# Attention probabilities turned in 32x32 blocks on VectorE and moved by DMA, and the first half of the output weights in units of two k tiles

## The chip, the cores and the metric

The kernel runs on one core of a Trainium2 chip. The metric is the device time of one execution in microseconds (us). Before the change it is 920.57 us, the median of three runs that lie between 920.27 and 920.67.

## The reference

The program is an encoder trunk of two equal layers over 256 positions and 1024 channels, all in float32. A layer is a feed-forward part, a mixer, and a second feed-forward part, each added to the residual stream `x`. Only the mixer is touched:

```
h    = rms_norm(x)
q, k, v, u, g = split(h @ w_in)                  # 5 x 512 columns
a    = dilated_attention(rotary(q), rotary(k), v)  # 8 heads of 64
sg   = gelu(u) * (w_s @ layer_norm(gelu(g)) + b)   # 4 groups of 128 channels, chunks of 128 positions
x    = x + concat(rms_norm(a), rms_norm(sg)) @ w_out   # w_out: 1024 x 1024
```

The kernel computes the three dilated windows of the attention as one softmax over 256 keys with a bias per pair of positions (the log of how many of the windows contain the pair, or -1e30).

## The kernel before

**Weights.** All weight matrices come from memory as one stream of units. A unit is 4 tiles of 128x512, 1 MB; `weight_units` lists them in the order of use. `load_unit` (line 119) loads a unit by one DMA on SyncE's queue into one of three `raw` buffers. `split_unit` makes two parts of it: ScalarE writes the high part `whi` (line 133), VectorE the rest `wlo` (line 134), in two pieces of 128x1024 each. `run_ahead`, called by every `multiply`, issues loads five units ahead and splits two units ahead. A load waits until the split of the unit three before it has read its buffer.

**Products.** The activations are split in the same way into `xTh` and `xTl`. `multiply` (lines 165 to 167) takes one unit: for each of its 4 k tiles and each of the two halves `t` of the positions it issues three matmuls, high by high, high by low and low by high, so 24 for a unit, into two PSUM banks of 128x512. Its argument `among` puts other work in front of the k tile of a given index.

**The order of work.** The kernel is written with a planner: instructions are listed in program order, and a list scheduler puts them on the engines' queues, earlier ones first, later ones where an earlier one isn't ready by its own estimate of the times. Each engine then runs its queue strictly in order. Semaphores for all dependences are put in by the planner, those of the DMAs included: a DMA on SyncE's queue that waits for its data holds up all DMAs behind it.

**The mixer.** `mixer` runs per layer through

1. q, k and v, one w_in unit of each and then the other; `rotate` and `turn_qk` prepare the transposed q and k.
2. g: at index 2 of its first unit `attend(0)`, at index 1 of its second `attend(1)`. Each handles four heads: `scores` (line 565 on) into two PSUM banks, bias and maximum on VectorE (L571), exponential on ScalarE (L580), and the division by the sum on VectorE (L583). The probabilities lie in `pr[a]` with the query positions on the partitions.
3. u: `turn_probs(0)` at index 1 of its first unit. It turns the keys onto the partitions by 16 transposes of 128x128 on TensorE (L596) into four PSUM banks `pt`, which VectorE (L598) and ScalarE (L600) copy out in turn to `prT`. `turn_probs(1)` stands at index 0 of u's second unit, `values(0)` and `normalise` at index 1, `values(1)` at index 3.
4. `values(a)` multiplies `prT` by v (L627, `pav`), and ScalarE (L632) and VectorE (L633) make of it `aT`, high and low part, two k tiles of the attention's output; ScalarE squares it into `sq` (L635). `normalise` is the Gelu and layer norm of g, whose result is `vv`.
5. The output product. w_out has 8 k tiles, 0 to 3 of the attention and 4 to 7 of the gating branch, and two column halves `d`. Its units are (rows 0 to 3, d = 0), (rows 0 to 3, d = 1), (rows 4 to 7, d = 0), (rows 4 to 7, d = 1). The products `oa` of the first two use `aT`; among them stand `gate` (L690: `vv` by the spatial weights, then `sg`), `square_sums` (L673) and `turn_sg`, 8 transposes of 128x128 on TensorE. The products `os` of the last two use `sgT`. `add` (L705) scales each by its branch's inverse root and adds it to `x_sb`.

PSUM has two pools of four banks: `ps_acc` for accumulators, `ps_sc` for all the rest. In SBUF the pool `big` has one buffer to a tag: `h0` to `h5`, which the feed-forward parts use for their hidden activations, serve the mixer as `qk` (h0), `qkh` and later `aT` (h1), the two `pr` (h2, h3), the two `prT` (h4, h0), `qkl` (h5) and `sgT` (h2).

The feed-forward parts already turn their hidden activations without TensorE: `turn_blocks` (L276) uses VectorE's transpose of 32x32 blocks, four instructions for each quarter of the partitions, which write blocks of one partition group to another.

Of the kernel before, what the change touches and what calls it, by code (L numbers as in the profile page):

```python
# [10 lines left out]
F32 = mybir.dt.float32  # L11
# [37 lines left out]
def weight_units():  # L49
# [3 lines left out]
    for l in range(DEPTH):  # L53
        for f in ("ffn1", "mix", "ffn2"):
            if f == "mix":
# [4 lines left out]
                for rows in (range(4), range(4, 8)):  # L60
                    for d in (0, 1):
                        units.append((l, "w_out", rows, d))
# [25 lines left out]
def trunk_kernel(ctx: ExitStack, tc: tile.TileContext, ws, x, cxt, rows, sgw, ident, bias, rot, out):  # L88
# [80 lines left out]
    def multiply_first(accs, lhs):  # L169

        for i in range(len(accs)):
# [3 lines left out]
            for j, k in enumerate(UNITS[i][2]):  # L175
                xh, xl = lhs(k)
                wh, wl = hi[:, j * W:(j + 1) * W], lo[:, j * W:(j + 1) * W]
                for t in range(NT):
# [3 lines left out]
                    nc.tensor.matmul(accs[j][t], xl[:, s], wh, start=False, stop=False)  # L182

# [327 lines left out]
    def mixer(l, st, nxt):  # L511
# [31 lines left out]
        prT = [big.tile([P, 4, 2, S], F32, tag="h4", name="prT")]  # L543
# [47 lines left out]
        def turn_probs(a):  # L591
            for h in range(4):
                pt = ps_sc.tile([P, 2, S], F32, tag="sc", name="pt")
                for kt in range(2):
                    for t in range(NT):
                        nc.tensor.transpose(pt[:, kt, t * P:(t + 1) * P], pr[a][:, t, h, kt * P:(kt + 1) * P], id_sb)  # L596
                if h % 2:
                    nc.vector.tensor_copy(prT[a][:, h], pt)  # L598
                else:
                    nc.scalar.activation(prT[a][:, h], pt, AF.Copy)  # L600
# [13 lines left out]
        multiply(acc_g, st.lhs, True, False, {2: lambda: attend(0)})  # L614
        multiply(acc_g, st.lhs, False, True, {1: lambda: attend(1)})

# [4 lines left out]
        def values(a):  # L621
            bank = ps_sc.tile([P, 2, S], F32, tag="sc", name="pav")
            for p in range(2):
                for kt in range(2):
                    for j in range(2):
                        h = 2 * p + j
                        nc.tensor.matmul(bank[j * DH:(j + 1) * DH, p], vs[:, kt, (4 * a + h) * DH:(4 * a + h + 1) * DH],  # L627
                                         prT[a][:, h, kt], start=kt == 0, stop=kt == 1)
# [10 lines left out]
        prT.append(big.tile([P, 4, 2, S], F32, tag="h0", name="prT"))  # L639
        multiply(acc, st.lhs, True, False, {1: lambda: turn_probs(0)})  # L640
# [20 lines left out]
        def values_and_gate():  # L661
            values(0)
            normalise()

        multiply(acc, st.lhs, False, True, {0: lambda: turn_probs(1), 1: values_and_gate, 3: lambda: values(1)})
        nc.vector.tensor_tensor(sq[:, :2], sq[:, :2], sq[:, 2:], op=ALU.add)
        nc.vector.tensor_tensor(sq[:, 0], sq[:, 0], sq[:, 1], op=ALU.add)
# [151 lines left out]
```

## Time and profile before

| what | value |
|---|---|
| median of three runs | 920.57 us |
| the profiled execution | 922.07 us, its span 920.3 us |
| TensorE's granted clock, mean | 0.999 |
| TensorE busy | 912.4 us (99%) |
| VectorE busy | 751.1 us (82%) |
| ScalarE busy | 466.3 us (51%) |
| moved by DMA | 174.14 MB, 189 GB/s |
| mixer of the first layer, from its first u matmul to its first oa matmul | 236.23 to 254.84 us |

The span goes from the first to the last instruction. TensorE's matmuls are pipelined: a duration in the profile holds the way through the array too, and the next one starts before it ends, so the distance between starts is what a matmul costs. Times in a timeline count from the span's start. The second layer's mixer looks like the first's, 453 us later.

### The profile page before, as it was taken

The page shows a single profiled execution, that of the slowest core. Times are in us where ns is not written, and L with a number is a line of the kernel's source. Part 1 is how long each engine was busy: PE and PEld are TensorE (multiplying, and loading weights), DVE is VectorE, ACT ScalarE, POOL GpSimd, SP SyncE. Part 2 cuts the span into 40 slices and gives each one's busy share as a digit, 9 for nine tenths or more (in the row PEclk, how much of TensorE's full clock was granted, in tenths as well). Part 3 has the DMA queues.
Part 4 walks back from the last instruction along what each step waited for, and adds up shares of the span by engine and source line. Part 5 has one row for each costly group of instructions (what it writes and reads, how often), then busy time and mean ns, then how long its engine had stood idle before and what let it go on. Part 6 is the DMA issues. An engine that isn't in the chain of part 4 may idle for free.

```text
span 920.3 us, 11062 instructions
## 1 busy us (share of the span) xinstructions
PE 912.4 (99%) x4178; PEld 750.2 (82%) x4178; DVE 751.1 (82%) x1203; ACT 466.3 (51%) x654; POOL 21.5 (2%) x48
## 2 busy tenths in 40 slices
PE   9999999999999999999999999999999999999997
PEld 6888888888778888888888888888887888888886
DVE  6698996796789699896687998966887887998854
ACT  6544544356756544434445544445467545444440
POOL 0000000000010000000000000000000100000000
PEclk9999999999999999999999999999999999999999
DMA  8765555565334645646555555455543455565351
GB/s 330 297 259 183 187 201 205 187 217 192 138 113 175 215 141 206 219 147 237 192 197 177 192 213 191 152 209 208 201 140 135 164 202 183 183 210 200 126 195 47
DMA packets 26982, 174.14 MB, mean 189 GB/s; under 512 B 3120, under 2 KB 4272, under 8 KB 6960
## 3 DMA queue, kind: packets, MB, share of 16 engines
q1 hardware_dynamic: 26496, 172.86, 52.6%
q8 instruction: 33, 0.54, 0.2%
q10 hardware_dynamic: 432, 0.56, 0.2%
q14 instruction: 21, 0.17, 0.1%
HBM read 172.36 MB, written 1.05 MB: 188 GB/s over the span
## 4 chain that ended last, share of the span: by engine, by line
PE 97%; DVE 1%; issue 1%; ACT 0%; DMA 0%; POOL 0%; POOLq 0%; DVEq 0%
PE down L165 8%; PE down L166 8%; PE down L167 8%; PE gate L166 7%; PE up L166 7%; PE up L167 7%; PE gate L167 7%; PE up L165 7%; PE gate L165 7%; PE both L166 2%; PE both L165 2%; PE both L167 2%; PE g L165 1%; PE q L167 1%; PE g L166 1%; PE os L165 1%
## 5 line engine op out<-in xcount | busy, mean ns | idle before, releaser
L134 DVE TENSOR_TENSOR wlo<-raw,whi 128x1024 fp32r<-128x1024 f32 (+2 forms) x325 | 378.4, 1201 | 105.1 <-ACT whi L133 102.8
L133 ACT ACTIVATE whi<-raw 128x1024 fp32r<-128x1024 f32 (+2 forms) x325 | 322.4, 1039 | 246.9 <-issue 100.1
L276 DVE STREAM_TRANSPOSE turned<-h 32x256 f32<-32x256 f32 (+1 forms) x384 | 158.9, 414 | 6.3
L167 PE MATMUL down<-whi,hT 128*128 128x512 f32 x340 | 132.3, 389 | 0.0
L165 PE MATMUL down<-whi,hT 128*128 128x512 f32 x340 | 132.3, 389 | 0.0
L166 PE MATMUL down<-wlo,hT 128*128 128x512 f32 x340 | 132.3, 389 | 0.0
L167 PE MATMUL gate<-whi,xTl 128*128 128x512 f32 x304 | 118.3, 389 | 0.0
L167 PE MATMUL up<-whi,xTl 128*128 128x512 f32 x304 | 118.3, 389 | 0.0
L166 PE MATMUL gate<-wlo,xTh 128*128 128x512 f32 x304 | 118.3, 389 | 0.0
L165 PE MATMUL up<-whi,xTh 128*128 128x512 f32 x304 | 118.3, 389 | 0.0
L166 PE MATMUL up<-wlo,xTh 128*128 128x512 f32 x304 | 118.3, 389 | 0.0
L165 PE MATMUL gate<-whi,xTh 128*128 128x512 f32 x304 | 118.1, 389 | 0.0
L167 PEld LDWEIGHTS down<-whi,hT 128*128 128x128 f32 x340 | 63.8, 188 | 13.3
L165 PEld LDWEIGHTS down<-whi,hT 128*128 128x128 f32 x340 | 63.8, 188 | 13.3
L166 PEld LDWEIGHTS down<-wlo,hT 128*128 128x128 f32 x340 | 63.8, 188 | 13.2
L279 ACT ACTIVATE hT<-turned 128x512 fp32r<-128x512 f32 x44 | 26.8, 626 | 80.2 <-DVE turned L276 80.2
L165 PEld LDWEIGHTS gate<-whi,xTh 128*128 128x128 f32 x304 | 57.1, 188 | 11.9
L165 PEld LDWEIGHTS up<-whi,xTh 128*128 128x128 f32 x304 | 57.1, 188 | 11.9
L166 PEld LDWEIGHTS up<-wlo,xTh 128*128 128x128 f32 x304 | 57.1, 188 | 11.9
L166 PEld LDWEIGHTS gate<-wlo,xTh 128*128 128x128 f32 x304 | 57.1, 188 | 11.9
L167 PEld LDWEIGHTS up<-whi,xTl 128*128 128x128 f32 x304 | 57.1, 188 | 11.8
L167 PEld LDWEIGHTS gate<-whi,xTl 128*128 128x128 f32 x304 | 57.0, 188 | 11.8
(172 smaller groups left out, 1064.7 us busy)
## 6 DMA issues: line engine op xcount, KB each, us to landing
raw<-in_ws SPq DMA_DIRECT2D x154, 1024.0 KB, 4.8
raw<-in_ws SPq DMA_DIRECT2D x8, 512.0 KB, 3.2
raw<-in_ws SPq DMA_DIRECT2D x7, 256.0 KB, 5.5
x_sb<-in_x SPq DMA_DIRECT2D x1, 1024.0 KB, 10.8
ln_sb<-in_rows SPq DMA_DIRECT2D x1, 1024.0 KB, 7.4
out<-y SPq DMA_DIRECT2D x2, 320.0 KB, 2.5
xt_sb<-in_cxt SPq DMA_DIRECT2D x1, 512.0 KB, 7.9
sgw_sb<-in_sgw SPq DMA_DIRECT2D x1, 512.0 KB, 6.5
```

The source lines that it names most:

```text
L133: nc.scalar.activation(hi[:, s], raw[:, s], AF.Copy)
L134: nc.vector.tensor_tensor(lo[:, s], raw[:, s], f32(hi[:, s]), op=ALU.subtract)
L165: nc.tensor.matmul(acc[t], xh[:, s], wh, start=start and j == 0, stop=False)
L166: nc.tensor.matmul(acc[t], xh[:, s], wl, start=False, stop=False)
L167: nc.tensor.matmul(acc[t], xl[:, s], wh, start=False, stop=stop and j == len(ks) - 1)
L276: nc.vector.transpose(to[32 * c:32 * c + 32, :, :, b, :], frm[32 * b:32 * b + 32, :, :, c, :])
L279: nc.scalar.activation(dst_hi, src, AF.Copy)
```

## The change

The probabilities leave TensorE. `turn_probs(a)` is now two VectorE instructions, one for each half of the query positions, that transpose all 32x32 blocks of a 128x1024 tile in place of their partition group (`prB`), and 16 DMAs on SyncE's queue from SBUF to SBUF that carry blocks to the partition group where they belong: one DMA for each pair of source group `b` and target group `c`, 32 partitions of 2 KB. All of a half's DMAs need both VectorE instructions, and a product of `values` needs all 16. `turn_probs(0)` now stands in program order behind g's first unit, `turn_probs(1)` behind its second. `values` reads the probabilities as its moving operand in runs of 32 elements. The buffers change: `prB` in h4 and h0, `prT` in h2 and h3 (where `pr` was), `sgT` in h5.

The first half of w_out comes in two units of two k tiles by both column halves. `multiply_pairs` runs through such a unit: k and k + 1 for d = 0, then for d = 1. So both halves' accumulators are open together (all four banks of `ps_acc`), and k tiles 2 and 3, which depend on `values(1)`, are first used in the second of the two units.

The order among the products changes with it: `normalise` stands ahead of u's second unit, `values(0)` at index 3 of it, `gate` at index 2 of the first pair unit, `values(1)` at index 0 of the second, `turn_sg` at its index 1, `square_sums` with the attention's inverse root at its index 3. All four `add`s of `oa` come behind it, and the first `os` accumulators take banks of `ps_sc`.

```diff
@@ weight_units
-                for rows in (range(4), range(4, 8)):
-                    for d in (0, 1):
-                        units.append((l, "w_out", rows, d))
+                for k in (0, 2):
+                    units.append((l, "w_out_pair", ((k, 0), (k + 1, 0), (k, 1), (k + 1, 1)), 0))
+                for d in (0, 1):
+                    units.append((l, "w_out", range(4, 8), d))
@@ trunk_kernel
+    def multiply_pairs(accs, lhs, start, stop, among):
+        i = done["used"]
+        done["used"] += 1
+        run_ahead(i + 1)
+        hi, lo = splits.pop(i)
+        for j, (k, d) in enumerate(UNITS[i][2]):
+            if j in among:
+                among[j]()
+            xh, xl = lhs(k)
+            wh, wl = hi[:, j * W:(j + 1) * W], lo[:, j * W:(j + 1) * W]
+            for t in range(NT):
+                s = slice(t * P, (t + 1) * P)
+                nc.tensor.matmul(accs[d][t], xh[:, s], wh, start=start and j % 2 == 0, stop=False)
+                nc.tensor.matmul(accs[d][t], xh[:, s], wl, start=False, stop=False)
+                nc.tensor.matmul(accs[d][t], xl[:, s], wh, start=False, stop=stop and j % 2 == 1)
@@ mixer
         def turn_probs(a):
-            for h in range(4):
-                pt = ps_sc.tile([P, 2, S], F32, tag="sc", name="pt")
-                for kt in range(2):
-                    for t in range(NT):
-                        nc.tensor.transpose(pt[:, kt, t * P:(t + 1) * P], pr[a][:, t, h, kt * P:(kt + 1) * P], id_sb)
-                if h % 2:
-                    nc.vector.tensor_copy(prT[a][:, h], pt)
-                else:
-                    nc.scalar.activation(prT[a][:, h], pt, AF.Copy)
+            tmp = big.tile([P, 4, 16, 32], F32, tag=("h4", "h0")[a], name="prB")
+            for t in range(NT):
+                nc.vector.transpose(tmp[:, :, 8 * t:8 * t + 8].rearrange("p c q j -> p q c j"),
+                                    pr[a][:, t].rearrange("p h (k c i) -> p (h k) c i", c=4, i=32))
+            dst = big.tile([P, 4, 16, 32], F32, tag=("h2", "h3")[a], name="prT")
+            for b in range(4):
+                for c in range(4):
+                    nc.sync.dma_start(dst[32 * c:32 * c + 32, b], tmp[32 * b:32 * b + 32, c])
+            prT.append(dst)
...
         multiply(acc_g, st.lhs, True, False, {2: lambda: attend(0)})
+        turn_probs(0)
         multiply(acc_g, st.lhs, False, True, {1: lambda: attend(1)})
+        turn_probs(1)
...
-                        nc.tensor.matmul(bank[j * DH:(j + 1) * DH, p], vs[:, kt, (4 * a + h) * DH:(4 * a + h + 1) * DH],
-                                         prT[a][:, h, kt], start=kt == 0, stop=kt == 1)
+                        probs = prT[a].rearrange("p b (t q) j -> p q t b j", t=NT)[:, 2 * h + kt]
+                        nc.tensor.matmul(bank[j * DH:(j + 1) * DH, p].rearrange("p (t b j) -> p t b j", t=NT, b=4),
+                                         vs[:, kt, (4 * a + h) * DH:(4 * a + h + 1) * DH], probs,
+                                         start=kt == 0, stop=kt == 1)
...
-        multiply(acc, st.lhs, True, False, {1: lambda: turn_probs(0)})
+        multiply(acc, st.lhs, True, False)
...
-        multiply(acc, st.lhs, False, True, {0: lambda: turn_probs(1), 1: values_and_gate, 3: lambda: values(1)})
+        normalise()
+        multiply(acc, st.lhs, False, True, {3: lambda: values(0)})
...
-        for d in (0, 1):
-            acc = accumulators("oa")
-            multiply(acc, a_lhs, True, True, {1: gate, 3: square_sums} if d == 0 else {0: turn_sg})
-            if d == 0:
-                r_a = inverse_root(ssq_a, DA)
-            add(acc, d, r_a)
+        accs = [accumulators("oa") for _ in range(2)]
+        multiply_pairs(accs, a_lhs, True, False, {2: gate})
+        r_a = []
+        def root_first():
+            square_sums()
+            r_a.append(inverse_root(ssq_a, DA))
+        multiply_pairs(accs, a_lhs, False, True, {0: lambda: values(1), 1: turn_sg, 3: root_first})
+        for d in (0, 1):
+            add(accs[d], d, r_a[0])
         r_s = inverse_root(ssq_s, DG)
         new = nxt()
         for d in (0, 1):
-            acc = accumulators("os")
+            acc = accumulators("os", ps_sc, "sc") if d == 0 else accumulators("os")
             multiply(acc, s_lhs, True, True)
```

The sums of `sq` move into `square_sums`, and the host's stream of weights gets the tiles of the pair units in their new order.

More of the change, by code (lines that the diff above doesn't have):

```diff
@@ L542, in mixer @@
         pr = [big.tile([P, NT, 4, S], F32, tag=f"h{2 + a}", name="pr") for a in range(2)]
-        prT = [big.tile([P, 4, 2, S], F32, tag="h4", name="prT")]
+        prT = []
         mx = small.tile([P, NT, 2, H], F32, tag="mx", name="mx")
@@ L638, in mixer @@
         acc = accumulators("u")
-        prT.append(big.tile([P, 4, 2, S], F32, tag="h0", name="prT"))
-        multiply(acc, st.lhs, True, False, {1: lambda: turn_probs(0)})
+        multiply(acc, st.lhs, True, False)
         vv = big.tile([P, NT, W], F32, tag="vv", name="vv")
@@ L659, in normalise @@
                                                op0=ALU.mult, op1=ALU.add)
-        def values_and_gate():
-            values(0)
-            normalise()
-        multiply(acc, st.lhs, False, True, {0: lambda: turn_probs(1), 1: values_and_gate, 3: lambda: values(1)})
-        nc.vector.tensor_tensor(sq[:, :2], sq[:, :2], sq[:, 2:], op=ALU.add)
-        nc.vector.tensor_tensor(sq[:, 0], sq[:, 0], sq[:, 1], op=ALU.add)
+        normalise()
+        multiply(acc, st.lhs, False, True, {3: lambda: values(0)})
         ssq_a = small.tile([P, NT, 1], F32, tag="ssq_a", name="ssq_a")
         def square_sums():
+            nc.vector.tensor_tensor(sq[:, :2], sq[:, :2], sq[:, 2:], op=ALU.add)
+            nc.vector.tensor_tensor(sq[:, 0], sq[:, 0], sq[:, 1], op=ALU.add)
             bank = ps_sc.tile([P, NT, 1], F32, tag="sc", name="ss")
@@ L681, in mixer @@
         sg = big.tile([P, NT, W], F32, tag="sg", name="sg")
-        sgT = big.tile([P, 2, 4, S], F32R, tag="h2", name="sgT")
+        sgT = big.tile([P, 2, 4, S], F32R, tag="h5", name="sgT")
         ssq_s = small.tile([P, NT, 1], F32, tag="ssq_s", name="ssq_s")
@@ L754, in _stream @@
                      for cc in range(2) for m in ("_w_gate", "_w_up")]
+            parts.append(np.concatenate(tiles, axis=1).reshape(-1))
+            continue
+        if name.endswith("_pair"):
+            tiles = [inputs[name[:-5]][l][k * P:(k + 1) * P, d * W:(d + 1) * W] for k, d in ks]
             parts.append(np.concatenate(tiles, axis=1).reshape(-1))
```

## The prediction

> **What bounds the kernel now.** I read the profile's page first, then the chain of waits in order of time through the first layer's mixer, then the timelines of TensorE, VectorE, ScalarE and SyncE there. Page:
>
> ```profile
> span 920.3 us, 11062 instructions
> ...
> PE 912.4 (99%) x4178; PEld 750.2 (82%) x4178; DVE 751.1 (82%) x1203; ACT 466.3 (51%) x654; POOL 21.5 (2%) x48
> ...
> PE 97%; DVE 1%; issue 1%; ACT 0%; DMA 0%; POOL 0%; POOLq 0%; DVEq 0%
> ```
>
> TensorE is busy 99% of the span and 97% of the chain that ends last is its own work. So an instruction taken off TensorE is worth its share of the stream, and any new wait in front of TensorE costs its full length. In the mixer the chain goes through the lines of the change (start, length, what):
>
> ```profile
> 237.76 1.75 PE pt L596 x16
> ...
> 243.60 1.75 PE pt L596 x16
> ...
> 246.72 1.88 PE pav L627 x16
> 248.60 0.43 PE u L165
> ...
> 258.54 1.96 PE mixed L690 x8
> ```
>
> Two blocks of 16 probability transposes (L596) stand on the chain in this layer, 1.75 us each; the product with the values (L627) takes 1.88, and the matmul behind it 0.43 instead of 0.23, so 2.08 in all.
>
> **What is removed.** The timeline of TensorE (start, duration, which overlaps the next one's):
>
> ```profile
> 236.23 0.39 PE L165 MATMUL u<-whi,xTh 128*128 128x512 f32 x1
> ...
> 237.36 0.39 PE L167 MATMUL u<-whi,xTl 128*128 128x512 f32 x1
> 237.60 1.91 PE L596 MATMUL pt<-id_sb,pr 128*128 128x128 f32 x16
> 239.26 0.48 PE L165 MATMUL u<-whi,xTh 128*128 128x512 f32 x1
> 239.57 0.40 PE L166 MATMUL u<-wlo,xTh 128*128 128x512 f32 x1
> ...
> 243.21 0.39 PE L167 MATMUL u<-whi,xTl 128*128 128x512 f32 x1
> ...
> 258.02 0.39 PE L167 MATMUL oa<-whi,aT 128*128 128x512 f32 x1
> ```
>
> and of the tile pt (duration min/median/max, first and last start):
>
> ```profile
> L596 PE MATMUL pt<-id_sb,pr x64: 270/272/273, 237.6 to 698.1; 128*128 128x128 f32 x64
> ```
>
> From 239.57 to 243.21 there are 16 steps of projection matmuls, 0.2275 each. From 237.36 to 239.57 are 2.21 us, of which two steps (0.455) would be there without the block: a block costs 1.755. The 64 transposes are four such blocks over two layers: **7.0 us off TensorE**. The duration of one, 272 ns, isn't its price; they overlap. The Trainium skill ("TensorE: Matmul & The Clock Gate", Part 4) gives about 275 ns for a transpose in a kernel's context; the trace has that duration, but a start every 0.104 us. Priced by that figure the gain would be 64 x 0.275 = 17.6 us, by the trace 7.0.
>
> Second, between 258.02 and 258.54 the gate's product (L690) starts 0.29 later than a step, because vv is late; in layer 2:
>
> ```profile
> 711.65 1.96 PE L690 MATMUL mixed<-vv,sgw_sb 128*128 128x256 f32 x8 [0.18 <-DVE vv L658]
> ```
>
> normalise now stands ahead of values(0) instead of behind it, so ScalarE gets to the Gelu of g sooner. I take these 0.47 us as gained too (bounds 0 and 0.47): **7.5 us** before new waits, 3.75 a layer.
>
> **What is added on VectorE.** Groups by line and shape (busy, mean ns):
>
> ```profile
> L276 DVE STREAM_TRANSPOSE turned<-h 32x256 f32<-32x256 f32 x320 | 139.6, 436 | 5.2
> ...
> L276 DVE STREAM_TRANSPOSE turned<-h 32x128 f32<-32x128 f32 x64 | 19.4, 303 | 1.1
> ...
> L598 DVE COPY prT<-pt 128x512 f32<-128x512 f32 x8 | 5.3, 681 | 0.0
> ```
>
> 128 more elements a partition cost 133 ns, so the new 128x1024 transpose takes an estimated 303 + 7 x 133 = 1.23 us; a layer has four (4.9 us) in place of four copies (2.6). TensorE doesn't feel this work itself, but it delays the probabilities:
>
> ```profile
> 232.51 1.22 DVE L583 TENSOR_TENSOR pr<-pr,sm 128x1024 f32<-128x1024 f32 x1
> 233.64 2.35 DVE L134 TENSOR_TENSOR wlo<-raw,whi 128x1024 fp32r<-128x1024 f32 x2
> ...
> 241.51 1.22 DVE L583 TENSOR_TENSOR pr<-pr,sm 128x1024 f32<-128x1024 f32 x1
> 242.66 2.35 DVE L134 TENSOR_TENSOR wlo<-raw,whi 128x1024 fp32r<-128x1024 f32 x2
> ```
>
> The first half's probabilities are normalised at 233.64. With one transpose behind them they are turned at 234.9, with both in the way at 236.1; I take 235.6, since VectorE has little idle time here. The second half's, at 242.66 now, get four transposes more ahead of them and two copies (1.28) fewer: 242.66 + 4.9 - 1.3 = 246.3; with a weight split of 2.35 slipped in, 248.6. I take 247.0.
>
> **What is added on SyncE's queue.** 16 DMAs of 64 KB for each half, and each reads both transposes, so all wait for the second. The issues of SyncE at the start, where they go back to back, and two of the mixer's:
>
> ```profile
> 0.72 1.81 SPq L119 DMA_DIRECT2D raw<-in_ws  x4
> 2.57 0.43 SPq L223 DMA_DIRECT2D xt_sb<-in_cxt  x1
> ```
>
> ```profile
> 236.02 0.33 SPq L119 DMA_DIRECT2D raw<-in_ws  x1
> 245.04 3.20 SPq L119 DMA_DIRECT2D raw<-in_ws  x2
> ```
>
> Four issues in 1.85 us are 0.46 each: the sixteenth starts 6.9 us after the first. Time from issue to landing, by kind:
>
> ```profile
> raw<-in_ws SPq DMA_DIRECT2D x154, 1024.0 KB, 4.8
> ...
> out<-y SPq DMA_DIRECT2D x2, 320.0 KB, 2.5
> ...
> raw<-in_ws SPq DMA_DIRECT2D x2, 128.0 KB, 3.3
> ...
> id_sb<-in_ident SPq DMA_DIRECT2D x1, 64.0 KB, 10.1
> ```
>
> No row moves SBUF to SBUF. The bounds are 2.5 (the stores at the end, nothing behind them) and 10.1 (64 KB as here, but issued into the crowd of the start). DMA share (last but one column) where they will run:
>
> ```profile
> 230.00:235.00 5.00, 5.00 (x40) 4.02 (x39) 4.80 (x11) 3.61 (x10) 0.00 (x0) 1.00 0.02 7
> 240.00:245.00 5.00, 5.00 (x31) 4.32 (x30) 4.97 (x8) 4.86 (x10) 0.00 (x0) 1.00 0.05 15
> ```
>
> The engines are nearly idle, so I take 2.9, between the store and the 128 KB load. The Trainium skill ("DMA: Bandwidth & Descriptors", Rules for kernel authors) speaks against transfers this small: under 64 KB one pays mostly overhead. Its fit for GpSimd's path, 2.0 us and bytes over 436e3, would make 2.15 us of one; with that the forecast below would be 914.3.
>
> **What waits behind it.** On SyncE the weight load of 236.02 now stands behind the first 16 (to about 242.9), that of 245.04 perhaps behind the second 16 (254.7). Landing in 4.8 they are there by 247.7 and 259.5. They are the second pair of w_out units, first used when the oa products end (about 265, below, and a unit later), and their split takes 2.35: both have over 2 us in hand, so I price them at nothing. If that cover were gone, each would cost its lateness one for one.
>
> **The path to the end of a layer's mixer.** Without the blocks TensorE reaches values(0), now at index 3 of u's second unit, after 42 steps: 236.23 + 42 x 0.2275 = 245.8. The last DMA starts at 235.6 + 6.9 = 242.5 and lands at 245.4 (bounds 245.0 and 252.6): just in time. Then 2.08 and 6 steps (249.2), a pair unit of 24 steps with the gate's 1.96 (256.7), and values(1), now first in the second pair unit. Its last DMA starts at 247.0 + 6.9, plus 0.4 for a weight load between, 254.3, and lands at 257.2: **0.5 us of wait** (0.1 at 2.5, 2.4 at 4.8). A wait at values(0) moves the need of values(1) too, so the two don't add.
>
> Behind values(1) stands its own consumer. Now:
>
> ```profile
> 248.65 0.47 ACT L632 ACTIVATE aT<-pav,cols_sb 128x256 fp32r<-128x256 f32 x1 [1.98 <-PE pav L627]
> ...
> 249.68 0.47 ACT L632 ACTIVATE aT<-pav,cols_sb 128x256 fp32r<-128x256 f32 x1 [0.55 <-DVE aT L633]
> ```
>
> ```profile
> 249.16 0.48 DVE L633 SCALAR_TENSOR_TENSOR aT<-pav,cols_sb,aT 128x256 fp32r<-128x256 f32 x1 [0.68 <-ACT aT L632]
> ```
>
> pav ends at 248.60; aT's high part is there at 249.12, its low part at 249.64, 1.0 later. Now six matmuls of u stand between; in the new order the next matmul uses k = 2 at once. turn_sg's 8 transposes (8 x 0.11 = 0.9) can fill it if the planner puts them there: 0.2 of wait filled, 1.0 not, I take **0.6**.
>
> The unit order of w_out, the adds of sq put later, sgT in h5 and os in the other PSUM pool add no instruction to TensorE; VectorE's four adds of oa come together at its end (4 x 0.7), under os' 24 steps (5.5). The values' moving operand is read in runs of 32 elements: at nothing, at worst twice its 1.88.
>
> Sum: 7.5 - 2 x (0.5 + 0.6) = 5.3 us. The span is 920.3 of a profiled execution of 922.07; the median of the runs is 920.57, near the span, and I take the 5.3 off the median: **915.3**.
>
> **Rivals.** *All hidden* (0.22): landing within 2.4, and the sg transposes fill the gap: 7.5 - 2 x 0.2 = 7.1, 913.5. For it: DMA shares of 0.02 and 0.05; against it: no row under 2.5.
> *VectorE is late* (0.14): the split goes ahead of the turn; 248.6 + 6.9 + 0.4 + 2.9 = 258.8, a wait of 2.1 and 1.0 for aT: 7.5 - 6.2, 919.3. For it: VectorE's 4.80 and 4.97 of 5 us.
> *The DMAs land late: slower* (0.15): values(1) waits for the sixteenth DMA. With 0.6 for aT the gain is gone when landing takes 2.4 + 3.15 = 5.5 us; midway between that and the 10.1 of the 64 KB row, at 7.8, the wait is 5.4, and 7.5 - 2 x 6.0 makes 925.1. For it: that row; against it: the idle engines.
> *The strided probabilities read slowly* (0.07): twice 1.88 in four products eats 7.5: 922.8. No row has runs of 32 on TensorE.
>
> **Numbers.** The forecast has 0.42 (its own range 914 to 917). The range goes from under the all-hidden case to past the slow reads, 912.5 to 923.0, and leaves out most of the late DMAs. Faster by over 0.2% (1.8 us, about what a measurement of this kernel tells from nothing): 0.42 and 0.22 and a third of VectorE late, 0.68; slower 0.19, same 0.13.
>
> **What would show it.** Right: L596 gone from TensorE and 4 x 1.75 from its stream; VectorE transposes of 128x1024 near 1.23 us; 16 issues some 7 us long on SyncE; TensorE idle before pav for about half a microsecond with DMA prT as releaser, and before oa for aT. Wrong: an idle of over 3 us before pav (late DMAs or VectorE: the time of the last transpose tells which), pav blocks longer than 1.88, or a wait for whi or wlo that points to starved weight loads.

## The result, and the profile after

The changed kernel takes 928.05 us (median of four executions, 927.62 to 929.3) beside 920.53 of the kernel before on the same chip: a ratio of 1.0084, 95% interval 1.0067 to 1.0102. The change makes it slower by 7.5 us, where 5.3 us faster was forecast. All times below are medians of undisturbed executions: of the ten of no_wait_for_move two, of 1009 and 2904 us, are left out. The profiled execution took 928.06. That of before had lost 1.8 us already in its first 10 us, so its span of 920.3 is too long for a comparison by spans (926.3 after); stages are compared instead. From the first matmul of u to the first of the feed-forward part behind it, the first layer's mixer takes 44.91 us before and 48.74 after, the second layer's 44.93 and 48.88. That stretch holds the whole loss.

The page of the changed kernel:

```profile
span 926.3 us, 10996 instructions
...
PE 908.0 (98%) x4114; PEld 744.6 (80%) x4114; DVE 755.4 (82%) x1203; ACT 462.5 (50%) x646; POOL 21.4 (2%) x48
```

The 64 transposes are gone (4178 matmuls before, 4114 now), yet the span grew. What TensorE waits for (in all, times, longest; the first six of the list, both layers; the third is of the start and stands in the list of before too):

```profile
PE oa L200 <- DVE aT L657: 5.3, 2, 2.7
PE oa L198 <- ACT aT L656: 2.6, 4, 0.8
PE sink L364 <- DVE warm L361: 1.2, 1, 1.2
PE pt L307 <- DVE x_sb L725: 1.0, 2, 0.5
PE pav L650 <- DVE st L673: 0.8, 1, 0.8
PE pav L650 <- DMA prT<-prB: 0.8, 1, 0.8
```

Without the line of the start these are 10.5 us, all of it new. The longest, 2.7 us a layer, is for the low part of aT, the step behind the first values. The timelines of TensorE and of VectorE there (start, duration, in brackets the idle time before it and its releaser):

```profile
246.22 1.95 PE L650 MATMUL pav<-prT,v 128*64 128x256 f32 x16 [0.76 <-DMA prT<-prB]
248.73 0.50 PE L198 MATMUL oa<-whi,aT 128*128 128x512 f32 x1 [0.56 <-ACT aT L656]
...
252.63 0.73 PE L200 MATMUL oa<-whi,aT 128*128 128x512 f32 x2 [2.71 <-DVE aT L657]
```

```profile
246.92 1.19 DVE L135 TENSOR_TENSOR wlo<-raw,whi 128x1024 fp32r<-128x1024 f32 x1
248.97 0.75 DVE L681 SCALAR_TENSOR_TENSOR vv<-vn,rs,ln_sb 128x512 f32<-128x512 f32 x1 [0.86 <-POOL rs L677]
249.64 0.75 DVE L679 SCALAR_TENSOR_TENSOR vn<-vn,mv,ln_sb 128x512 f32<-128x512 f32 x1
250.31 1.22 DVE L135 TENSOR_TENSOR wlo<-raw,whi 128x1024 fp32r<-128x1024 f32 x1
251.44 0.74 DVE L681 SCALAR_TENSOR_TENSOR vv<-vn,rs,ln_sb 128x512 f32<-128x512 f32 x1
252.10 0.48 DVE L657 SCALAR_TENSOR_TENSOR aT<-pav,cols_sb,aT 128x256 fp32r<-128x256 f32 x1
```

No matmul of u stands between the values and their consumer. The planner put u's last k tile ahead of the values. It probably took the moved probabilities to come later, by its own estimate: in three kernels below whose moves start earlier (four_moves_gate_later, no_transposes, all_relieved) that k tile stands behind the values again, in a fourth (no_division) it doesn't. No run tests this order alone. aT's high part is there at 248.67; the low part waits in VectorE's queue behind the layer norm's end, a wait for GpSimd inside it, and a weight split. VectorE has no slack to be on time. Windows of 4 us (busy time of PE, PEld, DVE, ACT, POOL, with the number of instructions; then granted clock, DMA share and GB/s), after and then before, and VectorE's first instruction of before in its last window. By the first matmul of u (234.42 after, 236.23 before), the same stage comes 1.8 us later in before:

```profile
238.00:242.00 4.00, 4.00 (x19) 3.30 (x19) 4.00 (x8) 3.78 (x14) 1.11 (x1) 1.00 0.44 100
242.00:246.00 4.00, 3.46 (x16) 2.53 (x14) 4.00 (x6) 3.99 (x6) 0.00 (x0) 1.00 0.48 107
250.00:254.00 4.00, 1.37 (x5) 0.94 (x6) 3.06 (x5) 1.39 (x3) 0.00 (x0) 0.95 0.46 114
```

```profile
238.00:242.00 4.00, 4.00 (x26) 3.56 (x25) 3.17 (x6) 4.00 (x14) 0.00 (x0) 1.00 0.53 225
250.00:254.00 4.00, 4.00 (x26) 2.56 (x25) 1.16 (x3) 3.43 (x6) 0.00 (x0) 1.00 0.47 199
```

```profile
253.32 1.28 DVE L650 BATCH_NORM_STATS2 st<-vn 128x6 f32<-128x512 f32 x2 [2.65 <-ACT vn L649]
```

Before, VectorE had caught up: it stood idle for 2.65 us up to 253.32, waiting for ScalarE, while TensorE went on without a gap (26 matmuls in the window). Now TensorE idles and waits for VectorE.

The wait also costs clock. Windows of 2 us of the changed kernel (granted clock third from the end):

```profile
252.00:254.00 2.00, 1.37 (x5) 0.94 (x6) 1.06 (x3) 1.39 (x3) 0.00 (x0) 0.91 0.45 107
254.00:256.00 2.00, 2.00 (x6) 1.52 (x6) 1.73 (x2) 1.47 (x3) 0.00 (x0) 0.50 0.44 99
256.00:258.00 2.00, 2.00 (x9) 1.70 (x7) 1.38 (x3) 0.00 (x0) 0.00 (x0) 0.74 0.43 98
```

Behind the idle 2.7 us the granted clock falls to 0.50, and a matmul starts every 0.425 us instead of 0.2275. From 253.20 to 258.24 stand seven matmuls and the gate's product, 5.04 us. At full clock they would be 7 x 0.2275 and 1.6 (its price before, without its wait for vv), 3.2 to 3.4 us: some 1.7 us are lost a layer. The windows give the same, 2 x (0.09 + 0.50 + 0.26).

SyncE's queue (start, time from first to last issue, count) and, on ScalarE, what comes of it:

```profile
234.57 10.09 SPq L619 DMA_DIRECT2D prT<-prB  x16
244.77 0.53 SPq L120 DMA_DIRECT2D raw<-in_ws  x1
245.77 11.06 SPq L619 DMA_DIRECT2D prT<-prB  x16
256.87 9.00 SPq L120 DMA_DIRECT2D raw<-in_ws  x4
```

```profile
262.06 2.01 ACT L134 ACTIVATE whi<-raw 128x1024 fp32r<-128x1024 f32 x2 [1.61 <-DMA raw<-in_ws]
263.97 0.46 ACT L656 ACTIVATE aT<-pav,cols_sb 128x256 fp32r<-128x256 f32 x1
```

The 16 issues take 10.1 and 11.1 us, and the next weight load goes out at 256.87. ScalarE waits for those weights at 262.06, and the high part of the second half's aT stands behind that split in ScalarE's queue: 0.65 us more of wait at 264.49.

By layer: 44.91 less the two blocks (3.51) and the late vv (0.29) would be 41.1, and it is 48.74. Of the 7.6 the waits of the first layer make 5.2 (0.76, 0.56, 2.71, 0.65, 0.52), the clock 1.7. Most of the remaining 0.7 went into the starts of the gating branch's transposes, now one block: they take 1.75 by the starts, 0.65 of it the wait, against 0.54 before.

### The profile page after: what moved, and what is told of

The parts are those of the page before. It is cut to its first block, busy times and chain, and to the rows that moved or that the text cites. A ratio compares the mean times of both kernels' runs of the same rounds, so it can differ in the third digit from the quotient of the medians.

```text
span 926.3 us, 10996 instructions
## 1 busy us (share of the span) xinstructions
PE 908.0 (98%) x4114; PEld 744.6 (80%) x4114; DVE 755.4 (82%) x1203; ACT 462.5 (50%) x646; POOL 21.4 (2%) x48
```

## The experiments

Four causes offer themselves: SyncE's issues and what stands behind them (A in the first texts), VectorE's queue (B), the new order in itself, and the late use of vv. The stretch given is that of the first layer, from u to the feed-forward part (before 44.91, after 48.74). In four kernels the second layer's differs by more than 1 us: turn_only 51.55, no_division 47.95, after_lo_on_pool 54.19, four_moves_gate_later 45.63.

| kernel | us | ratio to before, 95% | stretch |
|---|---|---|---|
| order_only | 923.56 | 1.0035 (1.0021 to 1.0050) | 46.59 |
| turn_only | 930.72 | 1.0109 (1.0094 to 1.0124) | 48.76 |
| no_wait_for_move | 922.63 | 1.0021 (1.0011 to 1.0031) | 45.79 |
| aT_first | 931.28 | 1.0114 (1.0095 to 1.0133) | 50.06 |
| two_queues | 934.86 | 1.0159 (1.0144 to 1.0174) | 52.12 |
| four_moves | 923.90 | 1.0032 (1.0022 to 1.0042) | 46.51 |
| four_moves_gate_later | 924.22 | 1.0046 (1.0030 to 1.0063) | 46.97 |
| before_and_transposes | 923.20 | 1.0028 (1.0018 to 1.0038) | 46.37 |
| before_and_moves | 920.51 | 1.0001 (0.9992 to 1.0010) | 44.90 |
| no_transposes | 920.87 | 1.0008 (0.9998 to 1.0017) | 45.15 |
| no_division | 923.92 | 1.0031 (1.0019 to 1.0043) | 46.14 |
| all_relieved | 917.83 | 0.9974 (0.9964 to 0.9984) | 43.62 |
| after_lo_on_pool | 938.18 | 1.0192 (1.0177 to 1.0207) | 51.82 |
| before_lo_on_pool | 929.92 | 1.0100 (1.0085 to 1.0115) | 49.09 |
| first_by_dma | 920.38 | 1.0000 (0.9990 to 1.0010) | 44.87 |
| second_by_dma | 920.80 | 1.0004 (0.9994 to 1.0013) | 45.09 |
| old_first_by_dma | 921.05 | 1.0007 (0.9997 to 1.0016) | 45.20 |
| mixed_tuned | 917.77 | 0.9972 (0.9962 to 0.9983) | 43.53 |

### The two parts of the change, each alone

`order_only`: the new order and the pair units, with the probabilities turned by TensorE.

```diff
         def turn_probs(a):
-            tmp = big.tile([P, 4, 16, 32], F32, tag=("h4", "h0")[a], name="prB")
...
+            for h in range(4):
+                pt = ps_sc.tile([P, 2, S], F32, tag="sc", name="pt")
...
-        multiply(acc, st.lhs, True, False)
+        multiply(acc, st.lhs, True, False, {1: lambda: turn_probs(0)})
-        multiply(acc, st.lhs, False, True, {3: lambda: values(0)})
+        multiply(acc, st.lhs, False, True, {0: lambda: turn_probs(1), 3: lambda: values(0)})
```

> The probabilities are turned on TensorE as before the change and copied out by VectorE and ScalarE; the pair units and the whole new order behind them (normalise, values, gate, turn_sg, adds) are kept. Theory A (the time goes to the arrival of prT: 16 issues on one queue take 10 to 11 us a half): no wait for prT is left, so only the new order's small waits in the second pair unit remain: 920.5 + 2 x 0.9 = 922. Theory B (the time goes to VectorE's queue, where the end of normalise and a weight split stand ahead of the low part of aT): that order stays, but six matmuls of u now stand between pav and oa: about 1.3 us a layer of wait and no drop of the clock, 924 to 925. Theory C (the new order costs the time by itself, whoever turns the probabilities): the change's cost of some 15 us without its gain of 7, 935.

It costs 3.0 us. Its waits:

```profile
PE oa L200 <- DVE aT L653: 1.8, 2, 0.9
...
PE pt L307 <- DVE x_sb L721: 1.1, 2, 0.5
```

Nothing but what VectorE makes is late, and with no added load on VectorE: the order alone uses up the slack that its queue had.

`turn_only`: the DMA turning, with the old units and the old places of values, gate and square sums.

```diff
+                for rows in (range(4), range(4, 8)):
+                    for d in (0, 1):
+                        units.append((l, "w_out", rows, d))
...
-        multiply(acc, st.lhs, False, True, {3: lambda: values(0)})
+        multiply(acc, st.lhs, False, True, {1: values_and_gate, 3: lambda: values(1)})
```

> The turning by VectorE and DMA alone: the output weights keep their old units and the values, the gate and the square sums their old places. The new order alone cost 3.0 us (923.6 against 920.5). If the two parts add up, this kernel takes 928.0 - 3.0 = 925.0. If the turning is a gain that only the new order spoils (the forecast's own sum less what the order was to hide), it takes 914 to 918. If the new order was what hid part of the moves, as the forecast had it, it takes more than 928, up to 932: the values are due earlier and TensorE waits for the moved copy, 2 us or more a half.

It is slower than the whole change: TensorE waits for the moves of the second half, 2.5 us in the first layer and 3.5 in the second. So the new order does hide most of the moves, as the forecast had it (0.8 us of wait is left in the changed kernel, which is 2.7 us faster than this one), and the parts don't add: +3.0 and +10.2 alone, +7.5 together.

### SyncE's queue

`no_wait_for_move`: the values read `prB`; the moves run, and nothing waits for them.

```diff
-            prT.append(dst)
+            prT.append(tmp)
```

> The changed kernel, with all its transposes and moves, but the products read the tile that VectorE's transposes wrote (blocks not moved to their partitions), so they wait for no move; what it leaves out is that the moved copy is used. Bound on what the arrival of prT costs in all. Theory A: every wait up to the first oa goes, 7 us of transposes gained and some 1 us a layer lost behind values(1): 915 to 917. Theory B: TensorE reaches aT sooner, but VectorE's queue still holds its low part: 920 or more.

`two_queues`: every second move is issued by ScalarE.

```diff
-                    nc.sync.dma_start(dst[32 * c:32 * c + 32, b], tmp[32 * b:32 * b + 32, c])
+                    (nc.sync, nc.scalar)[c % 2].dma_start(dst[32 * c:32 * c + 32, b], tmp[32 * b:32 * b + 32, c])
```

> The changed kernel, but every second of the 16 moves of a half is issued by ScalarE instead of SyncE; the computation is complete. Theory A: a half's issues take about 5 us instead of 10 to 11, prT lands some 5 us sooner, the planner finds it ready within u, and the waits of the first half (0.9 for prT, 0.6 and 2.7 for aT, 1.8 of half clock a layer) go: 928 - 2 x 5.7 = 916.7. If the issue time belongs to something the two queues share, nothing changes: 928. Theory B: only the part of the wait that u's last matmuls cover goes, 920 to 922.

`four_moves`: one DMA of 128 partitions in place of four.

```diff
-                for c in range(4):
-                    nc.sync.dma_start(dst[32 * c:32 * c + 32, b], tmp[32 * b:32 * b + 32, c])
+                nc.sync.dma_start(dst[:, b], tmp[:, b])
```

> Each half is moved by 4 DMAs of 128 partitions in place of 16 of 32; the bytes are the same, but no block changes its partitions, so the values are multiplied by a wrongly turned copy and the numbers that come out are not the reference's; the amount of work is the same. If SyncE's 32 issues a layer are the root (10.1 and 11.1 us in which the weight loads stand behind them), they take 4 x 0.59 = 2.4 us a half now, the moved copy comes 7 us sooner, the next weight loads too, and the time is 914 to 918. If VectorE's queue is the root (the copy without any wait for the move took 922.8), the time is 921 to 925, with 2 to 3 us a layer in which TensorE waits for a tile of VectorE. If it is the bytes and not the count that makes an issue long, an issue takes 2 us or more and the time stays at 927 to 929.

`four_moves_gate_later`: besides, `gate` stands behind the whole first pair unit.

```diff
-        multiply_pairs(accs, a_lhs, True, False, {2: gate})
+        multiply_pairs(accs, a_lhs, True, False, {})
+        pair_end = last[0]
...
+                    with tc.issue_after(pair_end):
+                        nc.tensor.matmul(bank[:, g], sgw_sb[:, l, g0 + g, :], vv[:, :, s], start=True, stop=True)
```

> The kernel with 4 moves a half (923.9; the moved blocks stay on their partitions, so the values are multiplied by a wrongly turned copy, with the same amount of work), and the gate's product put behind all 24 products of the first pair of output weights. There TensorE waited 2.9 us a layer for vv, its only long wait. If SyncE's issues and the place of the gate are together the whole loss, the 5.7 us go and the time is 916 to 919. If VectorE is late with whatever comes next, TensorE waits for the low parts of aT or for the turned gate instead, and the time is 921 to 925.

In the order no_wait_for_move, two_queues, four_moves and four_moves_gate_later, the first line of each list of waits, and between them ScalarE's queue in two_queues and SyncE's in four_moves:

```profile
PE mixed L710 <- DVE vv L681: 5.7, 2, 2.9
```

```profile
PE mixed L710 <- DVE vv L681: 13.5, 2, 6.8
```

```profile
234.92 5.38 ACTq L619 DMA_DIRECT2D prT<-prB  x8
240.35 0.51 ACT L598 ACTIVATE pr<-pr,mx 128x256 f32<-128x256 f32 x1 [8.20 <-DMA prT<-prB]
```

```profile
PE mixed L709 <- DVE vv L680: 5.7, 2, 2.9
```

```profile
235.38 2.47 SPq L618 DMA_DIRECT2D prT<-prB  x4
```

```profile
PE oa L202 <- DVE aT L658: 6.5, 2, 3.2
```

An issue costs 0.6 us by the count, not by the bytes (4 of 256 KB in 2.47). With the issues gone or the moves free the loss shrinks to 2 to 4 us and doesn't vanish: TensorE then waits 2.9 us a layer for vv, and with the gate out of the way 3.2 us for the low part of aT. These are two instructions of the same stretch of VectorE's queue. In two_queues TensorE no longer waits for the moves, which go out in 5.4 us instead of 10.1. But ScalarE's eight issues stand ahead of the exponentials of the second half, which start 3.1 us later than in the changed kernel, counted from u's first matmul (5.59 against 2.52), and the next eight take 5.0 us of its queue once more. In the end vv is 6.8 us late, and the kernel is slower than either account had allowed. On this the Trainium skill ("DMA: Bandwidth & Descriptors", Issuing engines are not separate DMA queues) says that issuing from several engines saves only the sequencer's time, usually small beside the transfer. For one move that is so here, 0.6 us against 2.0 from issue to landing; it is the 16 in a row, 10.1 us, that count, and on ScalarE they delay its compute.

`before_and_moves`: the kernel before with 32 unused moves a layer at the same places.

```diff
+            src = pr[a].rearrange("p t h s -> p (t h s)").rearrange("p (c q j) -> p c q j", c=4, j=32)
+            for b in range(4):
+                for c in range(4):
+                    nc.sync.dma_start(scr[b // 2][32 * c:32 * c + 32, b % 2], src[32 * b:32 * b + 32, c])
```

> The kernel before, with the 32 moves of 64 KB of each layer added on SyncE's queue, at the places where the changed kernel has them; they copy blocks of the probabilities to places that nothing reads. TensorE's work and VectorE's are as before, so only SyncE's queue and the transfers show: some 20 us of issues a layer ahead of the weight loads. If the weight loads behind them are in time all the same (priced at nothing in the prediction), 920.3 to 921. If these loads are what comes late, 922 to 927, with waits of ScalarE's split for its weights and of TensorE behind it.

In the old order SyncE's 21 us a layer cost nothing measurable, and no product of the mixer waits for weights.

### VectorE's queue

`aT_first`: in the changed kernel the end of the layer norm is issued behind the first half's low parts.

```diff
+                with tc.issue_after(low[1]):
+                    nc.vector.scalar_tensor_tensor(vn[t], vn[t], mv[:, t, 0:1], ln_sb[:, l, 0],
+                                                   op0=ALU.subtract, op1=ALU.mult)
```

> The changed kernel, with one thing moved: on VectorE's queue the end of normalise (the four instructions that make vv) stands behind the low part of the first half's aT instead of ahead of it. Turning, moves, units and TensorE's list up to the first oa are the same. Theory B: the wait of 2.7 us a layer ahead of the first high-by-low matmul of oa falls to about 0.4, and with it the time at half clock (about 1.8 us a layer): 928 - 2 x 4.1 = 920. Theory A: prT comes as late as before, and the wait only turns up elsewhere (vv and the gate are later): 926 to 928.

The wait of 2.7 is gone, and the time is worse, outside every outcome that was named. Its waits, and ScalarE in the second half:

```profile
PE oa L198 <- ACT aT L658: 7.4, 4, 3.3
PE pav L652 <- DMA prT<-prB: 4.1, 3, 1.8
```

```profile
261.91 2.00 ACT L134 ACTIVATE whi<-raw 128x1024 fp32r<-128x1024 f32 x2 [3.71 <-DMA raw<-in_ws]
```

TensorE gets to the second values earlier and meets SyncE's lateness there: the moves, and the weight split in front of aT. One queue put right exposes the other.

`before_and_transposes`: the kernel before with the eight block transposes a layer, unused.

```diff
+            for t in range(NT):
+                nc.vector.transpose(scr[t].rearrange("p c (g q) j -> p q (c g) j", g=2),
+                                    pr[a][:, t].rearrange("p h (k c i) -> p (h k) c i", c=4, i=32))
```

> The kernel before, with the eight block transposes of VectorE of each layer added at the places where the changed kernel has them; what they write is not used. TensorE's work and SyncE's are as before, so only VectorE's added load shows: 4 x 1.24 = 5.0 us a layer, half of it ahead of the end of g. If TensorE doesn't feel VectorE's queue (as the prediction had it), 920.3 to 921. If VectorE's queue is the root of the loss, 923 to 927, with new waits for tiles of VectorE behind u (the transposed probabilities, vv, aT).

2.6 us, but not in the way expected: in the mixer TensorE waits 0.2 us at most. By the starts on TensorE, u takes 0.53 us more in the first layer, the transposes 0.46, os 0.53. The planner cut TensorE's turns into more pieces (12, 4, 3, 9 and 4 instead of 16 and 16), presumably since it saw the probabilities later. So VectorE's 5 us a layer cost 1.3 us a layer even here, by the order and not by a wait.

`no_transposes`: the changed kernel without VectorE's transposes; the moves read `pr`. `no_division`: the division by the sums is left out instead, as much of VectorE. In both `gate` stands behind the first pair unit.

```diff
-            for t in range(NT):
-                nc.vector.transpose(tmp[:, :, 8 * t:8 * t + 8].rearrange("p c q j -> p q c j"),
-                                    pr[a][:, t].rearrange("p h (k c i) -> p (h k) c i", c=4, i=32))
+            tmp = pr[a].rearrange("p t h s -> p (t h s)").rearrange("p (c q j) -> p c q j", c=4, j=32)
```

> The changed kernel without VectorE's block transposes: the 16 moves a half copy the probabilities as they lie, so the values are multiplied by a copy that is turned only by blocks; the rest of the work is the same, and the gate's product stands behind the first pair of output weights. VectorE has 4 x 1.24 = 5.0 us a layer less, SyncE's 32 issues and the transfers stay. If VectorE's queue is the root, TensorE's waits for the low parts of aT go (2.7 us a layer) and with them the lowered clock (1.8 us a layer): 914 to 919. If SyncE's issues or the latency of the moves are the root, TensorE still waits for them: 923 to 928.

```diff
-            nc.vector.tensor_tensor(pr[a][:, t], pr[a][:, t], sm[:, t, 1, s][:, :, None].to_broadcast([P, 4, S]),
-                                    op=ALU.mult)
```

> The changed kernel without the division of the probabilities by their sums (4 x 1.22 = 4.9 us of VectorE a layer), all else the same, the gate's product behind the first pair of output weights. VectorE's relief lies at another place than in the kernel without the transposes, and the moves start earlier by one division. If it is VectorE's load that counts and not what VectorE does, 914 to 919 again. If it is the transposes themselves or the moves behind them, 923 to 928.

Waits of the first and of the second, and ScalarE in no_transposes:

```profile
PE oa L200 <- ACT aT L655: 3.4, 2, 1.7
PE oa L202 <- DVE aT L656: 2.5, 2, 1.2
```

```profile
PE oa L200 <- ACT aT L656: 6.0, 4, 2.5
PE oa L202 <- DVE aT L657: 2.0, 2, 1.0
```

```profile
256.91 0.63 ACT L277 ACTIVATE junk<-sg 128x512 f32<-128x512 f32 x1 [4.72 <-DVE sg L713]
...
258.16 1.99 ACT L134 ACTIVATE whi<-raw 128x1024 fp32r<-128x1024 f32 x2
```

Taking 5 us a layer off VectorE gives back 7.2 or 4.1 us, not the 9 to 14 expected. Of the waits that remain, half in the first kernel and two thirds in the second are for the high part of aT, which ScalarE makes behind a weight split. In no_transposes that split, at 258.16, waits for no weights: in ScalarE's queue it stands behind the squares of the gating branch, for which ScalarE idles 4.72 us. In no_division it waits 0.47 us for weights, too. So this is mostly the order of ScalarE's queue, as the planner set it, and only a little of it SyncE's lateness.

`all_relieved`: no transposes, and four moves a half, so both queues are relieved and the order is left. (Here the planner also puts the split ahead of those squares, and the wait for the high part is 0.2 us.)

> The changed kernel without VectorE's transposes and with 4 moves a half, which copy the probabilities as they lie (the values are multiplied by an unturned copy; the products, their sizes and their order stay), the gate's product behind the first pair of output weights. VectorE's 5 us a layer and most of SyncE's issues are gone together; only the new order is left. If these three are the whole loss, the time is 920.5 - 7.0 + 3.0 = 916.5, within 1.0: the 7.0 of the transposes left out and the 3.0 that the order alone cost. Of the waits of the kernel without transposes, the 1.7 us a layer for the high parts of aT behind a late weight split are gone. If something else is lost, 919 or more.

917.83: 1.3 above the sum, just outside what was given. The first halves' low part is still 1.2 us late a layer, and x_sb 0.5. From the changed kernel there are two ways to this one. By VectorE first, the 10.2 us split into 7.2 and 3.0 for SyncE; by SyncE first (924.2), into 3.8 and 6.4 for VectorE. These shares aren't pure. Leaving the transposes out also lets the moves start 5 us earlier; both routes move the gate behind the pair unit on their first step, which between four_moves and four_moves_gate_later changed nothing clear. The step of 6.4 is the cleanest, since TensorE waits for moves on neither side of it, and the low part's wait falls from 3.2 to 1.2 us. As much work taken off elsewhere in VectorE's queue (no_division) gave only 4.1. So VectorE's transposes are the larger share, 6.4 to 7.2 us, but where in its queue the work stands matters as much as how much it is.

### VectorE's work on GpSimd

`after_lo_on_pool` and `before_lo_on_pool`: the low parts of u's weights are made by GpSimd (the first with `gate` behind the first pair unit too).

```diff
-            nc.vector.tensor_tensor(lo[:, s], raw[:, s], f32(hi[:, s]), op=ALU.subtract)
+            eng = nc.gpsimd if UNITS[i][1] == "w_in" and UNITS[i][3] == 3 else nc.vector
+            eng.tensor_tensor(lo[:, s], raw[:, s], f32(hi[:, s]), op=ALU.subtract)
```

> The changed kernel with the low parts of the weights of u (4 of 128x1024 a layer, 4 x 1.22 = 4.9 us of VectorE) made by GpSimd, the gate's product behind the first pair of output weights; nothing is left out. No row shows what one of these takes on GpSimd. If VectorE is the root and GpSimd takes under 3 us for one, 914 to 920. If GpSimd takes over 4 us for one, the exponentials of the second half, whose negated maxima stand behind two of them, come late, and the time is over 928. If VectorE is not the root, 925 to 929.

> The kernel before with the same low parts of the weights of u made by GpSimd. If TensorE is what bounds the kernel before, as the prediction had it (waits of VectorE under 0.5 us a layer), the time stays at 920 to 921. If GpSimd is slow enough to hold up the exponentials, it is over 922. Below 919 VectorE was felt before too.

GpSimd's groups and ScalarE's timeline in the first:

```profile
L136 POOL TENSOR_TENSOR wlo<-raw,whi 128x1024 fp32r<-128x1024 f32 x8 | 21.0, 2653 | 71.5 <-ACT whi L134 71.5
```

```profile
238.56 0.51 ACT L601 ACTIVATE pr<-pr,mx 128x256 f32<-128x256 f32 x1 [5.10 <-POOL mx L598]
```

2.65 us for one, under the 3 that was to be enough, but two of them stand ahead of the negated maxima, and ScalarE idles 5.1 us ahead of the exponentials (0.27 in the changed kernel). Counted from u's first matmul they start 0.9 us later than there; in the other kernel 2.5 later than before. One division on VectorE beside GpSimd's work also took 3.44 us instead of 1.22. The kernels are 10.1 and 9.4 us slower than those they are made from; how much of it is GpSimd's queue was not taken apart. They say nothing on VectorE's share.

### Mixed kernels

Half of the heads by VectorE and DMA, half by TensorE: `first_by_dma` and `second_by_dma` in the new order, `old_first_by_dma` in the old one with the old units.

```diff
-        turn_probs(1)
...
-        multiply(acc, st.lhs, False, True, {3: lambda: values(0)})
+        multiply(acc, st.lhs, False, True, {2: lambda: turn_on_pe(1), 3: lambda: values(0)})
...
-        multiply_pairs(accs, a_lhs, True, False, {2: gate})
+        multiply_pairs(accs, a_lhs, True, False, {1: lambda: values(1), 3: gate})
```

> A mixed kernel: the first half of the heads is turned by VectorE and DMA, the second by TensorE as before, among the last k tiles of u; the values of the second half come among the first pair of output weights, the gate behind them. It saves 32 transposes a layer, 3.5 us in all, and has 16 moves a layer. If the second 16 moves are what delays the weight loads and with them the second half, the time is 917 to 921. If VectorE's queue is the root, TensorE waits 1 to 3 us a layer for the low parts of aT or for vv all the same, and the time is 921 to 926.

> The other mixed kernel: the first half by TensorE among the first k tiles of u, the second by VectorE and DMA, with its values at the end of the first pair of output weights. It saves the same 3.5 us. The first values no longer wait for a move, and the second have 8 us more. If the early moves of the first half were what hurts, the time is 917 to 920; if the load on VectorE hurts wherever it lies, or the weight loads behind the 16 moves that are left do, it is 922 to 927.

> The old units and the old order, with the first half of the heads turned by VectorE and 16 moves a layer, and the second half by TensorE as before. It leaves out 32 transposes in all, 3.5 us. If the moves of the first half (done by 246.8, where the kernel before starts these values at 246.7) and VectorE's 2.5 us a layer are hidden, the time is 916 to 918. If VectorE or the weight loads behind the moves are felt, the gain is eaten: 920 to 923.

All three end where the kernel before is: 3.5 us of transposes gained and lost again. In first_by_dma one wait is left, and it is VectorE's queue once more: the low part of aT at 251.55 stands behind two splits and a copy from PSUM, TensorE idles for 1.06 us. `mixed_tuned` is that kernel with the end of the layer norm behind the first low part, and one of the two copies of the second half moved to ScalarE:

```diff
-                if h % 2:
+                if h == 1:
                     nc.vector.tensor_copy(dst[:, h], pt)
...
+                with tc.issue_after(low[0]):
+                    nc.vector.scalar_tensor_tensor(vn[t], vn[t], mv[:, t, 0:1], ln_sb[:, l, 0],
+                                                   op0=ALU.subtract, op1=ALU.mult)
```

> The mixed kernel that turns the first half by VectorE and DMA (920.4), with VectorE's queue put in order: the end of the normalisation behind the first low part of aT, and one more of the copies of the second half from PSUM on ScalarE instead of VectorE. There TensorE waited 1.06 us a layer for that low part, its only long wait. If that wait goes and nothing takes its place, the time is 920.4 - 2.1 = 918.3, faster than both kernels by over 0.2%. If vv, which now comes later, holds up the gate's product instead, the time is 920 or more.

VectorE in its first layer:

```profile
245.21 2.33 DVE L135 TENSOR_TENSOR wlo<-raw,whi 128x1024 fp32r<-128x1024 f32 x2
249.92 0.48 DVE L675 SCALAR_TENSOR_TENSOR aT<-pav,cols_sb,aT 128x256 fp32r<-128x256 f32 x1 [2.38 <-ACT aT L674]
250.32 0.74 DVE L701 SCALAR_TENSOR_TENSOR vn<-vn,mv,ln_sb 128x512 f32<-128x512 f32 x1
```

The low part is made as soon as its input is there, TensorE has no wait left in the mixer, and the kernel takes 917.77 us: faster than the kernel before by 2.7 us (0.9972, 0.9962 to 0.9983) and than the change as it was by 10.3. It changes two things on VectorE's queue at once; which of them counts more isn't shown.

## Why the prediction was wrong

Forecast 915.3, range 912.5 to 923.0; measured 928.05. What held:

- "7.0 us off TensorE": the blocks are gone, and the gate's product no longer waits for vv.
- The transpose of 128x1024: 1.24 us against an estimated 1.23; turned at 234.5 and 245.6. Counted from u's first matmul that is 0.7 and 0.4 us later than taken.
- Landing: 2.0 us against 2.9. The strided reads cost nothing: the values' products take 3.76 us a layer by their starts in four_moves and 3.75 before. So the rivals of slow reads and of late landings fell, the second for the reason given against it, the idle DMA engines.

What failed, by its steps:

- **"TensorE doesn't feel this work itself."** This is the main one. VectorE's added work was followed only to the probabilities. What stands behind it in VectorE's queue (vn, vv, splits, the low part of aT) was never dated, although VectorE's 4.80 and 4.97 of 5 us were quoted. Measured: 2.7 us a layer of wait for that low part, with the clock behind it. By the kernels without transposes the work cost 6.4 to 7.2 us; as much taken off elsewhere (no_division) gave 4.1. The rival "VectorE is late" had it late for the turn of the probabilities only.
- **"Then 2.08 and 6 steps" and "I take 0.6".** The u matmuls that were to cover aT's conversion were moved ahead of the values by the planner, and the wait was taken from a VectorE that was free. Measured: 0.56 and 2.71 at the first half, 0.65 at the second. That the last is near 0.6 is luck: the high part was late because it stood behind a late weight split. The order alone, at unchanged load, costs 3.0 us, where the forecast had a gain of 0.47 in it and no other price.
- **"Four issues in 1.85 us are 0.46 each."** These moves take 0.589 us each (median), 0.63 from start to start, so the sixteenth starts 9.5 and 10.5 us after the first, not 6.9. values(0), which was to be "just in time", waited 0.76 us for it; the 0.5 us forecast at values(1) didn't occur, since TensorE came later.
- **"I price them at nothing"**, of the weight loads. Right in the old order (before_and_moves: no loss), wrong here: the split waited 1.61 us, in aT_first 3.71, and ScalarE's next work, the second half's aT, with it. The two ways to all_relieved put SyncE at 3.0 to 3.8 us, the moves and the weights together.
- The clock was not priced at all: some 1.7 us a layer behind the one wait of 2.7.

The rival on the slower side named one mechanism, the DMAs landing late. The loss came as a chain, each link of which was thought of as cover for another. Still open are the 1.3 us by which all_relieved lies above the sum of its parts, and how the 3.0 us of the order divide.

## What to carry to other kernels

An engine that is off the chain may still run without a gap for long (VectorE here for 20 us, from 227.97 to 248.11), and then each instruction added to it delays all that stands behind it: list its queue from the added work up to the next result that the bounding engine needs, and date each entry. When work is moved off the bounding engine, it also loses the cover under which the others caught up; here TensorE's transposes and the u matmuls behind the values were probably that cover, though no run takes it apart. When one wait is removed and the time doesn't fall, look which queue the next one comes from, and relieve both at once before judging either.

## What the runs showed of the hardware

- An idle of TensorE of 2.7 us was followed by a granted clock of 0.50 in the next 2 us, with 0.74 behind; one of 2.6 us in the second layer by 0.75 and 0.50. The Trainium skill ("TensorE: Matmul & The Clock Gate", Part 1, What's actually happening) gives an idle window of about 3.4 us for that; here the shorter one sufficed. Length alone doesn't decide: idles of 2.0 us between transposes (before_lo_on_pool) were followed by clocks of 0.54 and 0.61, while 3.2 us in the second layer of four_moves_gate_later left it at 1.00. What decides is open. The wait of 1.1 us in first_by_dma left the clock at 1.00.
- An SBUF to SBUF DMA costs its issuer about 0.6 us whether it carries 64 or 256 KB, on SyncE as on ScalarE, and both queues issue side by side without slowing each other (8 in 5.0 and 5.4 us).
- The moving operand of these products, read in runs of 32 floats, costs no more than a contiguous one (3.76 us a layer in four_moves against 3.75 before).
